# Output projection and query products from two-part operands, low weight parts by GpSimd, in a two-layer trunk on one core

## The chip, the core and the metric

The kernel runs on one core of a Trainium2 chip. The metric is the device time of one execution in microseconds (us), the median of several runs. Engines are named as in the profile: PE is TensorE's matrix product, PEld its weight load, DVE is VectorE, ACT is ScalarE, POOL is GpSimd, SP is SyncE, which issues most transfers. TensorE's granted clock is given as a share of full speed.

## What is computed

The input is 256 tokens of 1024 numbers, with 16 learned tokens in front: 272 tokens. Two layers follow, all in float32. In short:

```
def mixer(x):
    h = rmsnorm(x, mix_g);  z = h @ w_in                 # 1024 -> 3488
    y_conv = silu(layernorm(depthwise_conv31(glu(z)))) @ w_conv_out
    y_mla  = chunk_causal_attention(q, k, v) @ w_mla_out # 8 heads, 96 per head
    merged = sigmoid(g1) * y_conv + sigmoid(g2) * y_mla
    return x + merged @ w_out                            # output projection

def peer(hf):                                            # hf = rmsnorm(x, ffn_g)
    q = (hf @ wq).reshape(T, 8, 2, 128)                  # query products
    s = einsum('thpd,hpnd->thpn', q, keys)               # 128 keys per half
    sv, si = top_k(s, 16)                                # per half
    cand = sums of the two halves (16 x 16);  top_s, pos = top_k(cand, 16)
    ids = si[0] * 128 + si[1];  gw = softmax(top_s)      # 128 experts per token
    act = gelu(u_table[ids] . hf) * gw
    return sum over the 128 experts of act * v_table[ids]

for layer in range(2):
    x = mixer(x);  x = x + peer(rmsnorm(x, ffn_g))
return x[16:]
```

There are 128 x 128 = 16384 experts; `u_table` and `v_table` have 64 MB each per layer.

## The kernel before, in words

Activations stand transposed: 128 features on the partitions, tokens along the row, as `hT` with 8 chunks of 272 columns. In layer 1 the first 16 tokens are left out where they are no longer needed, so tiles have 256 columns there. The program's order on every engine is the order in which it is written; waits between engines are by semaphore. PSUM tiles named `z` rotate through 3 buffers, `sc` through 2.

Dense weights, and both expert tables, come as a stream of 1 MB transfers from SP into four buffers `wraw`; each holds two tiles of 128x1024, and `next_w` hands out the next one. A buffer is filled again when both of its tiles have been used.

The mixer ends with three groups of products. `half_tile(oo)` and `half_tile(uu)` form the attention's and the convolution's outputs; the latter's loop multiplies and adds the gates (L719, L720) into `xh`. Then come 8 tiles of the output projection: `ztile(t0, xh)` makes 8 products per tile over the 8 chunks (each product of two f32 operands is two instructions in the trace), VectorE adds the result to `hT` (L724), ScalarE forms `xg`, `hT` times a gain (`scaled`, L167), and a square (L171), VectorE adds up the squares (L173).

The query loop (16 tiles, from L889) multiplies `xg` with `wq`. ScalarE takes each tile out of PSUM as `qr` (L892). After tile i, TensorE makes the scores of tile i-1 with the keys, and VectorE finds their 16 best (`top16`, five passes, two rows of 128 scores per tile). After tile 1 VectorE computes the inverse norm (`rstd`, L266 and L154 to L159). In tiles 4 to 11 GpSimd multiplies one chunk of `xg` by it and so forms `xh` (L919), the operand of the expert products. From tile 9 on, VectorE works one step per tile at `second`, which finds the best 16 of the sums for the first four heads of the first 128 tokens. After the loop it does the next four heads; then the table `ew` of expert numbers goes out and GpSimd can issue the first gathers.

The experts are computed in two ways. For the last 160 tokens all experts are computed densely: 128 tiles `A` (this is the u stage), GELU, times a matrix `X` of weights that is built on the way from one-hot products (`wbuild`, 40 blocks of 4 tokens), then 128 tiles `po` with `v_table` (the v stage). For the first 96 tokens, and in layer 0 the 16 learned ones, u and v rows are gathered by expert number (1 MB per gather, 112 gathers in layer 0 and 96 in layer 1) and multiplied on VectorE (L1138, L1122).

In the u stage two side programs advance with the tiles: `gathers` by `RU` steps per tile, and `b_`, which runs the routing of the second 128 tokens and then `wbuild`. `b_` takes `RB` = 0.75 steps per tile while it routes, and `RW` steps per tile once it builds weights. In `routes`, `LAG` steps stand before four transposes (L1031) that turn `ef`, the expert numbers and weights, for `wbuild`; the second half of the tokens comes last.

Of the kernel before, what the change touches and what calls it, by code (L numbers as in the profile page):

```python
# [35 lines left out]
RB = 0.75  # L36
RW = (0.52, 0.47)
C_MIX, C_FFN, C_CW, C_CB, C_LG, C_LB, C_QA, C_KVA, C_QN, C_KN = 0, 8, 16, 140, 144, 148, 152, 154, 155, 156
# [5 lines left out]
def trunk_kernel(ctx: ExitStack, tc: tile.TileContext, a: dict, out: bass.AP, dbg=None, stop=None):  # L44
# [124 lines left out]
    def square(sq, c, c0):  # L169

        S.activation(sq[:, c, c0:], hT[:, c, c0:], AF.Square)  # L171
        if c:
            V.tensor_add(sq[:, 0, c0:], sq[:, 0, c0:], sq[:, c, c0:])  # L173

    carry = None
    for l in range(NL):
# [74 lines left out]
        def ztile2():  # L251

            ws = [next_w(), next_w()]
            ps = [zp.tile([128, 512], F32, name="z", bufs=3) for _ in range(2)]
            for c in range(8):
                for w_, p in zip(ws, ps):
                    mm(p[:, :T], w_[:, c * 128:(c + 1) * 128], xg[:, c], c == 0, c == 7)
            return [p[:, :T] for p in ps]

        def sums(dst, src, n):  # L260
# [451 lines left out]

        xh = pp.tile([128, 8, T], F32, name="xh")
        for i in range(4):
            ps = half_tile(uu)
            for f in range(2):
                c = 2 * i + f
                mg = mp.tile([128, T], F32, name="az", bufs=2)
                V.tensor_mul(mg[:, :TQ], gt[0][:, c, t0:], ps[f])  # L719
                V.tensor_add(xh[:, c, t0:], mg[:, :TQ], gt[1][:, c, t0:])  # L720
        xg, sq = big("xg", [8, T]), big("sq", [8, T])
        for i in range(8):
            p = ztile(t0, xh)
            V.tensor_add(hT[:, i, t0:], hT[:, i, t0:], p)  # L724
            scaled(xg, l, i, C_FFN, t0)
            square(sq, i, t0)
# [162 lines left out]
        for i in range(16):  # L889
            z = ztile(t0)  # L890
            qT_ = mp.tile([128, T], F32, name="qr", bufs=2)
# [25 lines left out]
            if 4 <= i < 12:  # L917
                c = i - 4
                G.tensor_tensor(xh[:, c, t0:], xg[:, c, t0:], rs, op=OP.mult)  # L919
        scores(15, pend)  # L920
# [83 lines left out]
        def routes():  # L1004
# [5 lines left out]
            for k in range(2):  # L1010
# [10 lines left out]
                if k == 0:  # L1021
                    if not last:
# [3 lines left out]
                        V.scalar_tensor_tensor(iww[-1].bitcast(I32)[:, 0, 0], im[:, 0], 128.0, im[:, 1], op0=OP.mult, op1=OP.add)  # L1026
                for _ in range(LAG + (7 if last and k == 0 else 0)):
                    yield
# [314 lines left out]
```

## Time and profile before

| | |
|---|---|
| median of 3 runs | 1809.7 us (1806.8 to 1811.29) |
| profiled execution | 1810.55 us, span 1808.8 us, mean granted clock 0.991 |
| PE busy | 1760.8 us (97%) |
| DVE, ACT, POOL busy | 1144.0 us (63%), 423.1 us (23%), 336.4 us (19%) |
| moved by DMA | 559.37 MB, mean 309 GB/s |

| stage | layer 0, from us | layer 1, from us |
|---|---|---|
| output projection | 198.15 | 1112.10 |
| u stage, expert products `A` | 303.08 | 1203.93 |
| routing out, first transfer `iww<-ew` | 321.10 | 1222.81 |

A row of the timeline gives start, length and engine, the line of the kernel and the operation, what is written and read, shape, count, and in brackets the idle time before it with what ended it. Rows of matrix products overlap at their ends, so the pace is read from starts. A row by form gives count, busy time and the mean length in ns. A busy TensorE is not one at its peak, since the length of a product is modelled.

### The profile page before, as it was taken

To read this page: it belongs to the slowest core of one execution; us is meant where nothing else is said; L and a number is where in the kernel's file an instruction comes from. 1 tells how busy PE (TensorE), PEld (TensorE's weight loads), DVE (VectorE), ACT (ScalarE), POOL (GpSimd) and SP (SyncE) were. 2 spreads that over 40 slices of the span, in tenths; PEclk is the share of its full clock that TensorE was granted. 3 is DMA by queue.
4 is the path that set the end of the run, shared out by engine and by line. 5 is a ranking of instruction groups with operands and counts; after the bars stand their busy time and mean duration, and the time that the engine had idled before them with its cause. 6 is when DMAs were issued, how large, how long until landed. Compare 5 with 4: busy or idle time off the path is not lost.

```text
span 1808.8 us, 29412 instructions
## 1 busy us (share of the span) xinstructions
PE 1760.8 (97%) x11611; PEld 1626.7 (90%) x11611; DVE 1144.0 (63%) x3101; ACT 423.1 (23%) x1233; POOL 336.4 (19%) x393
## 2 busy tenths in 40 slices
PE   9999999979999999999999999999899999999998
PEld 7678888979999999999996888899799999999998
DVE  5587358898888654544535764596878886444441
ACT  3443102324444100000014331132244431000000
POOL 0121010122111222333200220102211122322210
PEclk9999999989999999999999999999899999999999
DMA  6123433999999999999961224449999999999993
GB/s 228 70 94 117 157 123 141 367 373 423 424 423 424 424 424 421 424 422 417 422 232 70 94 103 153 163 161 382 366 424 424 423 423 418 421 412 402 421 412 146
DMA packets 80682, 559.37 MB, mean 309 GB/s; under 512 B 9176, under 2 KB 12120, under 8 KB 13080
## 3 DMA queue, kind: packets, MB, share of 16 engines
q1 hardware_dynamic: 49488, 338.54, 46.5%
q0 software_dynamic: 30336, 218.35, 29.1%
q8 instruction: 91, 1.49, 0.3%
q10 hardware_dynamic: 720, 0.60, 0.1%
q14 instruction: 47, 0.39, 0.1%
HBM read 556.18 MB, written 1.05 MB: 308 GB/s over the span
## 4 chain that ended last, share of the span: by engine, by line
PE 73%; DMA 15%; issue 6%; DVE 5%; ACT 0%; POOL 0%; SPq 0%; POOLq 0%; DVEq 0%; ACTq 0%
PE po L52 22%; PE A L52 21%; PE z L52 21%; DMA wraw<-vn 10%; PE aps L52 5%; DMA gb<-uv,iww 3%; PE wp L52 2%; DMA wraw<-u 1%; DVE va L1122 1%; DVE gb L1138 1%; DMA iww<-ew 0%; DVE ex L866 0%; PE xp L52 0%; PE sc L52 0%; DMA wraw<-w_in 0%
## 5 line engine op out<-in xcount | busy, mean ns | idle before, releaser
L52 PE MATMUL po<-X,wraw 128*128 128x160 f32 x4096 | 570.0, 300 | 14.7 <-DMA wraw<-vn 11.0
L52 PE MATMUL A<-xh,wraw 128*128 128x160 f32 x4096 | 580.9, 302 | 3.3 <-DMA wraw<-u 2.1
L52 PEld LDWEIGHTS po<-X,wraw 128*128 128x128 f32 x4096 | 557.8, 190 | 25.3 <-DMA wraw<-vn 20.3
L52 PEld LDWEIGHTS A<-xh,wraw 128*128 128x128 f32 x4096 | 563.3, 191 | 5.0 <-DMA wraw<-u 2.9
L1138 DVE SCALAR_TENSOR_TENSOR gb<-gb,xr 128x1024 f32<-128x1024 f32 x208 | 254.5, 1223 | 348.0 <-DMA gb<-uv,iww 347.6
L52 PE MATMUL z<-xg,wraw 128*128 128x272 f32 (+1 forms) x1408 | 336.3, 393 | 1.3 <-DMA wraw<-w_in 0.7
L1110 POOL DMA_INDIRECT gb<-uv,iww x208 | 217.4, 1045 | 541.5 <-DVE va L1122 366.1
L52 PEld LDWEIGHTS z<-xg,wraw 128*128 128x128 f32 x1408 | 264.7, 192 | 58.5 <-issue 7.2
L1122 DVE SCALAR_TENSOR_TENSOR va<-gb,am,va 128x1024 f32<-128x1024 f32 x203 | 261.2, 1287 | 7.2
L1148 ACT ACTIVATE am<-am 128x1 f32<-128x1 f32 x208 | 41.4, 199 | 598.2 <-DVE gb L1138 598.1
L1052 ACT ACTIVATE ohA<-ohE,wlo 128x128 f16<-128x128 f16 x320 | 105.4, 427 | 11.0 <-DVE ohE L1049 7.5
L1109 POOL COPY warm<-wraw 1x1 f32<-1x1 f32 x91 | 49.6, 545 | 286.0 <-DMA wraw<-vn 286.0
L577 POOL TENSOR_TENSOR acc<-acc,cp 128x272 f32<-128x272 f32 (+1 forms) x60 | 50.7, 845 | 276.4 <-ACT cp L576 274.1
L569 DVE SCALAR_TENSOR_TENSOR acc<-upad,cols,acc 128x272 f32<-128x272 f32 (+1 forms) x180 | 83.6, 520 | 0.2
L1062 ACT ACTIVATE X<-wp 128x356 f32<-128x356 f32 (+24 forms) x80 | 26.8, 335 | 169.6 <-DVE X L1059 164.7
L1049 DVE TENSOR_TENSOR ohE<-ioh,idxT 128x512 f16<-128x512 f16 x160 | 60.5, 419 | 0.0
L52 PE MATMUL z<-xh,wraw 128*128 128x272 f32 (+1 forms) x256 | 57.3, 386 | 0.0
L52 PEld LDWEIGHTS z<-xh,wraw 128*128 128x128 f32 x256 | 48.6, 190 | 8.3
L52 PE MATMUL wp<-ohE,ohA 128*128 128x128 f16 x640 | 49.9, 219 | 0.0
L52 PEld LDWEIGHTS <-ohA 128*128 128x128 f16 x640 | 43.3, 97 | 3.0
L919 POOL TENSOR_TENSOR xh<-xg,rq_ym 128x272 f32<-128x272 f32 (+1 forms) x16 | 11.3, 742 | 181.8 <-DVE sv L749 93.5
L1059 DVE SCALAR_TENSOR_TENSOR X<-wp,X 128x156 f32<-128x156 f32 (+24 forms) x80 | 38.3, 479 | 6.9 <-PE wp L52 6.6
(302 smaller groups left out, 1248.5 us busy)
## 6 DMA issues: line engine op xcount, KB each, us to landing
wraw<-u SPq DMA_DIRECT2D x128, 1024.0 KB
wraw<-vn SPq DMA_DIRECT2D x128, 1024.0 KB
wraw<-w_in SPq DMA_DIRECT2D x27, 1024.0 KB
wraw<-wq SPq DMA_DIRECT2D x16, 1024.0 KB
wraw<-w_out SPq DMA_DIRECT2D x8, 1024.0 KB
wraw<-w_mla SPq DMA_DIRECT2D x4, 1024.0 KB
wraw<-w_conv SPq DMA_DIRECT2D x4, 1024.0 KB
gb<-uv,iww POOLq DMA_INDIRECT x208
```

The lines of the kernel that those rows point to most:

```text
L52: PE.matmul(o, l, r, start=start, stop=stop, skip_group_check=True)
L569: V.scalar_tensor_tensor(acc[:, c, t0:], u_, weight(c, k), acc[:, c, t0:], op0=OP.mult, op1=OP.add)
L577: G.tensor_tensor(acc[:, 0, t0:], acc[:, 0, t0:], u_[:, t0:], op=OP.add)
L1049: V.tensor_tensor(E[q], ioh[:, None].to_broadcast(full), pairs(q, b), op=OP.is_equal)
L1052: S.activation(A_[1][:, t // 2, :, t % 2], E[0][:, t // 2, :, t % 2], AF.Copy, scale=wlo[:, 4 * b + t:4 * b + t + 1])
L1059: V.scalar_tensor_tensor(X[:, :J, s_], p[:, :, :J].rearrange("p t j -> p j t"), 1.0 / WS, X[:, :J, s_], op0=OP.mult, op1=OP.mult)
L1062: S.activation(X[:, J:, s_], p[:, :, J:].rearrange("p t j -> p j t"), AF.Copy, scale=1.0 / WS)
L1109: G.tensor_copy(warm[0:1], state["w"][0:1, 0:1])
L1110: G.indirect_dma_start(out=g_, out_offset=None, in_=a[f"uv{l}"], in_offset=bass.IndirectOffsetOnAxis(ap=iww[i].bitcast(I32)[:, m // 16, 0, ...
L1122: V.scalar_tensor_tensor(vac[i], r, m_, vac[i], op0=OP.mult, op1=OP.add)
L1138: V.scalar_tensor_tensor(u_, u_, 1.0, xrs[i], op0=OP.mult, op1=OP.mult, accum_out=m_)
L1148: S.activation(m_, m_, AF.Gelu_apprx_tanh)
```

## The change

The output projection and the query products are made by `ztile3` instead of `ztile`. Weights and activations are each split in a high part of type f32r (a float32 rounded to fewer bits by the write) and a low part, the rounded rest. A tile is then 24 products: for each chunk high weights with high and with low activations, and then low weights with high activations.

`split` makes the weights' parts two tiles ahead, in two buffers each: the high part is a copy by ScalarE (128x1024), the low part a subtraction by GpSimd (128x1024). The first two are made in the loop before the output projection, the others behind each tile, 24 in a layer. The activations' parts are made by ScalarE and VectorE: `mgh` and `mgl` from `xh` before the output projection, `xgr` and `xgl` from `hT` behind each of its tiles. The squares go to the buffer `acc` with 4 slots. In the query loop `xh` is now `hT` times the inverse norm on GpSimd, then times the gain on ScalarE (L957). `RW` becomes 0.56 in both layers, and the lag before the transposes 3 + 2 steps (layer 0) or 3 + 9 (layer 1) for the first half of the tokens and 3 + 5 for the second, where it was 3, and 3 + 7 for the first half in layer 1.

```diff
--- before.py
+++ after.py
@@ -34,7 +34,7 @@
 J0 = 8
 LAG = 3
 RB = 0.75
-RW = (0.52, 0.47)
+RW = (0.56, 0.56)
 C_MIX, C_FFN, C_CW, C_CB, C_LG, C_LB, C_QA, C_KVA, C_QN, C_KN = 0, 8, 16, 140, 144, 148, 152, 154, 155, 156
 N_COLS = 157
 QT = ((16, 128), (144, 128), (0, 16))
@@ -168,9 +168,10 @@
 
     def square(sq, c, c0):
 
-        S.activation(sq[:, c, c0:], hT[:, c, c0:], AF.Square)
+        b = c and 1 + (c - 1) % (sq.shape[1] - 1)
+        S.activation(sq[:, b, c0:], hT[:, c, c0:], AF.Square)
         if c:
-            V.tensor_add(sq[:, 0, c0:], sq[:, 0, c0:], sq[:, c, c0:])
+            V.tensor_add(sq[:, 0, c0:], sq[:, 0, c0:], sq[:, b, c0:])
 
     carry = None
     for l in range(NL):
@@ -256,6 +257,32 @@
                 for w_, p in zip(ws, ps):
                     mm(p[:, :T], w_[:, c * 128:(c + 1) * 128], xg[:, c], c == 0, c == 7)
             return [p[:, :T] for p in ps]
+
+        parts = []
+
+        def split():
+
+            w_ = next_w()
+            b = split.n % 2
+            split.n += 1
+            h, lo = split.hs[:, b], split.ls[:, b * 1024:(b + 1) * 1024]
+            S.activation(h, w_, AF.Copy)
+            G.tensor_tensor(lo, w_, h.bitcast(F32), op=OP.subtract)
+            parts.append((h, lo))
+
+        split.n = 0
+
+        def ztile3(xhi, xlo):
+            h, lo = parts.pop(0)
+            p = zp.tile([128, 512], F32, name="z", bufs=3)[:, :TQ]
+            for c in range(8):
+                mm(p, h[:, c * 128:(c + 1) * 128], xhi(c), c == 0, False)
+                mm(p, h[:, c * 128:(c + 1) * 128], xlo(c), False, False)
+            for c in range(8):
+                mm(p, lo[:, c * 128:(c + 1) * 128], xhi(c), False, c == 7)
+            if split.n < 24:
+                split()
+            return p
 
         def sums(dst, src, n):
             for c in range(n):
@@ -711,18 +738,28 @@
         uu = vt["u"]
 
         xh = pp.tile([128, 8, T], F32, name="xh")
+        mgh, mgl = big("xg", [8, T], F32R), big("sq", [8, T], F32R)
+        split.hs = mp.tile([128, 2, 8 * 128], F32, name="wuq").bitcast(F32R)
+        split.ls = mp.tile([128, 8, T], F32, name="kh").bitcast(F32R).rearrange("p a b -> p (a b)")
         for i in range(4):
             ps = half_tile(uu)
+            if i == 3:
+                split()
+                split()
             for f in range(2):
                 c = 2 * i + f
                 mg = mp.tile([128, T], F32, name="az", bufs=2)
                 V.tensor_mul(mg[:, :TQ], gt[0][:, c, t0:], ps[f])
                 V.tensor_add(xh[:, c, t0:], mg[:, :TQ], gt[1][:, c, t0:])
-        xg, sq = big("xg", [8, T]), big("sq", [8, T])
+                S.activation(mgh[:, c, t0:], xh[:, c, t0:], AF.Copy)
+                V.tensor_tensor(mgl[:, c, t0:], xh[:, c, t0:], mgh.bitcast(F32)[:, c, t0:], op=OP.subtract)
+        xgr, xgl, sq = big("g0", [8, T], F32R), big("g1", [8, T], F32R), acc
         for i in range(8):
-            p = ztile(t0, xh)
+            p = ztile3(lambda c: mgh[:, c, t0:], lambda c: mgl[:, c, t0:])
             V.tensor_add(hT[:, i, t0:], hT[:, i, t0:], p)
-            scaled(xg, l, i, C_FFN, t0)
+            scaled(xgr, l, i, C_FFN, t0)
+            V.scalar_tensor_tensor(xgl[:, i, t0:], hT[:, i, t0:], cl[:, C_FFN + i:C_FFN + i + 1],
+                                   xgr.bitcast(F32)[:, i, t0:], op0=OP.mult, op1=OP.subtract)
             square(sq, i, t0)
         if stop == f"mix{l}":
             dump(stop, hT)
@@ -887,7 +924,7 @@
         pend = None
         xh = pp.tile([128, 8, T], F32, name="xh")
         for i in range(16):
-            z = ztile(t0)
+            z = ztile3(lambda c: xgr[:, c, t0:], lambda c: xgl[:, c, t0:])
             qT_ = mp.tile([128, T], F32, name="qr", bufs=2)
             S.activation(qT_[:, t0:], z, AF.Copy)
             if i == 0:
@@ -916,7 +953,8 @@
                 next(early, None)
             if 4 <= i < 12:
                 c = i - 4
-                G.tensor_tensor(xh[:, c, t0:], xg[:, c, t0:], rs, op=OP.mult)
+                G.tensor_tensor(xh[:, c, t0:], hT[:, c, t0:], rs, op=OP.mult)
+                S.activation(xh[:, c, t0:], xh[:, c, t0:], AF.Copy, scale=cl[:, C_FFN + c:C_FFN + c + 1])
         scores(15, pend)
         if not last:
 
@@ -1024,7 +1062,7 @@
                         im = r2.tile([128, 2, 16], F32, name="im")
                         yield from second(mv, mi, 1, rsT[:, 2:3], im, iww[-1][:, :, 1])
                         V.scalar_tensor_tensor(iww[-1].bitcast(I32)[:, 0, 0], im[:, 0], 128.0, im[:, 1], op0=OP.mult, op1=OP.add)
-                for _ in range(LAG + (7 if last and k == 0 else 0)):
+                for _ in range(LAG + (5 if k else 9 if last else 2)):
                     yield
                 p = pW.tile([128, 512], F32, name="wp", bufs=2)
                 for q in range(4):
```

VectorE's rows of two output tiles in layer 0, before: `hT` is the residual stream, `sq` the squares.

```order
L719 TENSOR_TENSOR az<-g_603,z 128x272
L720 TENSOR_TENSOR xh<-az,g_604 128x272
L724 TENSOR_TENSOR hT<-hT,z 128x272 x2
L173 TENSOR_TENSOR sq<-sq 128x272
L724 TENSOR_TENSOR hT<-hT,z 128x272
```

The same place now; `g_1399` and `g_1400` hold the high and low parts of the next operand, `acc` the squares, `xg` and `sq` in the third row the parts of `xh`.

```order
L752 TENSOR_TENSOR az<-g_603,z 128x272
L753 TENSOR_TENSOR xh<-az,g_604 128x272
L755 TENSOR_TENSOR sq<-xh,xg 128x272
L759 TENSOR_TENSOR hT<-hT,z 128x272
L761 SCALAR_TENSOR_TENSOR g_1400<-hT,cols_61,g_1399 128x272
L759 TENSOR_TENSOR hT<-hT,z 128x272
L761 SCALAR_TENSOR_TENSOR g_1400<-hT,cols_61,g_1399 128x272
L174 TENSOR_TENSOR acc<-acc 128x272
```

One operation with two SBUF inputs is new per chunk before the projection, and one per tile in it.

GpSimd's rows from the convolution's last adds to the routing in layer 0, before:

```order
L110 IOTA io 128x128
L577 TENSOR_TENSOR acc<-acc,cp 128x272 x30
L919 TENSOR_TENSOR xh<-xg,rq_ym 128x272 x8
L928 DMA mv<-svm 64x1x16
L928 DMA mi<-sim 64x1x16
```

And now; `kh` holds the low weight parts, `wuq` the high ones.

```order
L110 IOTA io 128x128
L604 TENSOR_TENSOR acc<-acc,cp 128x272 x30
L270 TENSOR_TENSOR kh<-wraw,wuq 128x1024 x15
L956 TENSOR_TENSOR xh<-hT,rq_ym 128x272
L270 TENSOR_TENSOR kh<-wraw,wuq 128x1024
L956 TENSOR_TENSOR xh<-hT,rq_ym 128x272
```

The eight multiplications, which stood together, now stand singly behind a subtraction each.

ScalarE's rows in the query loop of layer 0, before, with `tx` a table for `second`:

```order
L171 ACTIVATE sq<-hT 128x272
L892 ACTIVATE qr<-z 128x272 x10
L811 ACTIVATE tx_1815<-it_1811 128x1024
L811 ACTIVATE tx_1817<-it_1812 128x1024
L892 ACTIVATE qr<-z 128x272 x3
```

And now, tiles 3 to 5:

```order
L929 ACTIVATE qr<-z 128x272
L269 ACTIVATE wuq<-wraw 128x1024
L929 ACTIVATE qr<-z 128x272
L957 ACTIVATE xh<-xh,cols_61 128x272
L269 ACTIVATE wuq<-wraw 128x1024
```

Each copy of high weight parts now stands behind the scaling of the tile before, which waits for GpSimd.

## Rows read from the trace of the kernel before

**Rows 1.** Busy time by engine in stretches; first line names the columns

```profile
core 0: us, PE busy (x) PEld busy (x) DVE busy (x) ACT busy (x) POOL busy (x), PEclk, DMA share, GB/s
...
360.00:380.00 20.00, 18.97 (x140) 18.49 (x139) 18.14 (x68) 4.59 (x8) 3.63 (x3) 1.00 1.01 423
...
380.00:400.00 20.00, 9.89 (x56) 8.92 (x55) 19.03 (x53) 5.34 (x13) 3.62 (x4) 0.71 0.87 351
...
1280.00:1300.00 20.00, 11.43 (x67) 10.48 (x67) 19.04 (x56) 5.02 (x13) 3.81 (x3) 0.74 0.80 325
...
640.00:700.00 60.00, 57.81 (x417) 56.12 (x416) 30.44 (x49) 3.38 (x13) 14.01 (x23) 1.00 1.01 421
...
1550.00:1600.00 50.00, 50.00 (x370) 50.00 (x369) 22.40 (x36) 1.83 (x9) 15.43 (x18) 1.00 1.01 422
...
235.92:320.44 84.52, 83.94 (x447) 70.16 (x447) 69.80 (x414) 14.44 (x31) 10.05 (x16) 1.00 0.38 138
```

**Rows 2.** TensorE in order of time: start, length, what, count, idle before

```profile
198.15 29.50 PE L52 MATMUL z<-xh,wraw 128*128 128x272 f32 x128
...
236.15 3.93 PE L52 MATMUL z<-xg,wraw 128*128 128x272 f32 x16
...
240.80 3.94 PE L52 MATMUL z<-xg,wraw 128*128 128x272 f32 x16
...
1112.10 27.79 PE L52 MATMUL z<-xh,wraw 128*128 128x256 f32 x128
...
1151.41 3.62 PE L52 MATMUL z<-xg,wraw 128*128 128x256 f32 x16
...
1155.31 3.62 PE L52 MATMUL z<-xg,wraw 128*128 128x256 f32 x16
```

**Rows 3.** TensorE around the first weight-building products of layer 0

```profile
405.97 0.62 PE L52 MATMUL wp<-ohE,ohA 128*128 128x128 f16 x8
...
406.43 4.56 PE L52 MATMUL A<-xh,wraw 128*128 128x160 f32 x32
```

**Rows 4.** TensorE in layer 1, the four transposes of the second token half

```profile
1290.80 0.45 PE L1031 MATMUL wp<-ident,ef 128*128 128x128 f32 x1 [4.02 <-DVE am L1117]
...
1294.73 0.48 PE L1031 MATMUL wp<-ident,ef 128*128 128x128 f32 x1 [3.48 <-DVE ef L867]
...
1296.27 0.80 PE L1031 MATMUL wp<-ident,ef 128*128 128x128 f32 x2 [1.07 <-DVE ef L1019]
...
1296.86 10.27 PE L52 MATMUL A<-xh,wraw 128*128 128x160 f32 x64
```

**Rows 5.** GpSimd: the multiplications by the inverse norm; below, by form

```profile
243.91 5.78 POOL L919 TENSOR_TENSOR xh<-xg,rq_ym 128x272 f32<-128x272 f32 x8 [93.51 <-DVE sv L749]
...
1155.52 5.51 POOL L919 TENSOR_TENSOR xh<-xg,rq_ym 128x256 f32<-128x256 f32 x8 [88.26 <-ACT qr L892]
...
L577 POOL TENSOR_TENSOR acc<-acc,cp 128x272 f32<-128x272 f32 x30 | 26.0, 868 | 123.1 <-ACT cp L576 122.2
```

**Rows 6.** GpSimd and VectorE at two moments of layer 0, single instructions

```profile
104.61 0.76 POOL L577 TENSOR_TENSOR acc<-acc,cp 128x272 f32<-128x272 f32 x1 [0.35 <-ACT cp L576]
...
104.61 1.06 DVE L569 SCALAR_TENSOR_TENSOR acc<-upad,cols,acc 128x272 f32<-128x272 f32 x1
...
91.67 0.76 POOL L577 TENSOR_TENSOR acc<-acc,cp 128x272 f32<-128x272 f32 x1 [10.13 <-ACT cp L576]
...
91.77 0.44 DVE L677 TENSOR_TENSOR g<-z,rq_ym 128x272 f32<-128x272 f32 x1 [2.41 <-PE z L52]
```

**Rows 7.** VectorE, first and last of the twelve inverse-norm steps, layer 0

```profile
238.31 0.42 DVE L266 TENSOR_SCALAR rq_x<-st 128x272 f32<-128x272 f32 x1
...
243.24 0.44 DVE L159 SCALAR_TENSOR_TENSOR rq_ym<-rq_w,rq_ym 128x272 f32<-128x272 f32 x1
```

**Rows 8.** ScalarE by form: count, busy us, mean ns of one

```profile
L976 ACT ACTIVATE xs<-xh 128x1024 f32<-128x1024 f32 x5 | 5.2, 1045 | 0.0
...
L167 ACT ACTIVATE xg<-hT,cols 128x272 f32<-128x272 f32 x24 | 11.4, 515 | 74.3 <-DVE hT L724 42.2 <-PE po L52 26.2 <-DMA hT<-hT 5.2
```

## The prediction

> **What bounds the kernel now.** I read the table of stretches first. In layer 0 the DMA engines are full from the first expert gathers to the end of the layer: 421 to 423 GB/s, also late, when TensorE has room (640 to 700 us: 417 instructions in 60 us; in layer 1 it does 370 in 50 us, which is its own pace) [rows 1]. So the end of layer 0 is the start of its gathers plus a fixed amount of bytes; the start of the gathers hangs on VectorE's routing, which follows the query products. In layer 1, with 96 gathers for 112, TensorE has no idle time late (50.00 of 50 us) [rows 1], and the end is when the expert products begin plus TensorE's work. In both layers the stage that the diff rewrites (output projection, query products, routing) is serial with what sets the end: a microsecond there is a microsecond of the kernel.
>
> Both layers also have a hole. Near 380 to 400 and 1280 to 1300 us TensorE is busy 9.89 and 11.43 of 20 us, its granted clock falls to 0.71 and 0.74, and the DMA rate drops to 351 and 325 GB/s [rows 1]: in layer 1 the transposes of the second token half wait 4.02, 3.48 and 1.07 us, mostly for VectorE's `ef` [rows 4].
>
> **The matmuls.** An output tile takes 29.34/8 = 3.67 us in layer 0 (27.79/8 = 3.47 in layer 1), as 16 instructions. A query tile with its scores goes every 4.65 us (240.80 - 236.15), in layer 1 every 3.90 [rows 2], so the scores take 0.98 and 0.43. After: 24 instructions per tile, each one part by one part. The trace has no such operand. Its upper neighbour is the f32 instruction of today, 3.67/16 = 229 ns; its lower one the f16 product, 0.46 us for 8 of 128 columns, 57.5 ns [rows 3], so 122 ns for 272 columns and 115 for 256. I take the lower one, since a part is meant to go through once, and keep the upper as a rival. A tile is then 24 x 122 = 2.93 us (2.76), 0.74 us (0.71) less than now, if it is fed. 24 tiles per layer would give 17 to 18 us.
>
> **What feeds them.** Per tile ScalarE copies 128x1024 (1.05 us, the row of `xs` [rows 8]) and GpSimd subtracts 128x1024. GpSimd's 272 and 256 columns take 5.78/8 = 0.722 and 5.51/8 = 0.689 us [rows 5], a slope of 2.06 ns per column; 752 more columns make 0.722 + 1.55 = 2.27 us. Ends: 2.0, if long rows go a little better than that slope; 3.27, the 868 ns of the convolution's adds [rows 5] scaled by 1024/272. I take 2.3, the nearest rows.
>
> That would fit under 2.9 us, but VectorE cannot work freely beside it. At 104.61 us a GpSimd add of 0.76 us and a VectorE operation with two SBUF inputs start together, and the latter takes 1.06 us; a VectorE operation with one input in PSUM, begun 0.10 us into another GpSimd add, takes 0.44 [rows 6]. The row shows 0.6 us lost beside a 0.76 us add, and that the wait ends when the add ends. I carry that over: beside a subtraction of 2.3 us such an operation waits up to 2.3 us, and everything behind it in VectorE's queue too.
>
> The Trainium skill, "SBUF — State Buffer", section "Who interferes with whom", says that a VectorE instruction with two SBUF inputs and a GpSimd instruction that reads SBUF take a shared port in turns, whoever is second waiting for the whole instruction of the other. With no more than the row's 0.6 us lost per subtraction, 24 of them would cost at most 14 us per layer and vanish in VectorE's idle time, and the time would be near the first rival's 1779; by the rule it is up to 2.3 us each, and the sum below. The trace agrees as far as its 0.76 us adds go.
>
> **Sum for layer 0.** (a) Output projection: per tile VectorE adds to `hT`, forms the low part (two SBUF inputs) and adds squares (two SBUF inputs), 0.45 us each by the inverse norm's steps, (243.24 - 238.31)/11 [rows 7]. With the subtraction, turn about: 2.3 + 3 x 0.45 = 3.65, and some 0.25 for the hops to ScalarE and back (estimate): 3.9 against 3.67, so +2 over 8 tiles instead of -6. The first two subtractions fall on the last `xh` and low-part operations, half hidden: +2. The first query tile needs the last low part, behind one more subtraction: +2. Together +6. (b) First four query tiles: 4 x -0.74 = -3. (c) The inverse norm: twelve steps, 5.4 us [rows 7], nine with two SBUF inputs. TensorE keeps ahead and a subtraction runs in each tile, four before it runs dry: 5.4 + 4 x 2.3 = 14.6 us. The first top-16 (2.4 us: 235.92 to 238.31) stands before it, the second behind: 19.4 us, and `scores(3)` needs the PSUM buffer that this second one reads. It is due after 3 x 3.91 = 11.7 us: +7. (d) Tiles 4 to 11: ScalarE's scaling of `xh` waits for GpSimd's multiplication, which stands behind the subtraction, which waits for ScalarE's copy, which stands behind the previous scaling. Once round: 1.05 + 2.3 + 0.72 + 0.5 (`xg`, 515 ns [rows 8]) + 0.3 for hops = 4.9 against 4.65: +2, less the two tiles split during the wait in (c): 0. The copies and subtractions end two tiles early; the last collide with the `second` steps, whose waits fill VectorE's idle time (84.5 - 69.8 = 14.7 us between first score and routing [rows 1]). Layer 0: +6 - 3 + 7 + 0 = +10 us, for TensorE and for the start of the gathers.
>
> **Sum for layer 1.** Fewer columns, faster tiles before, the same subtraction: (a) (3.9 - 3.47) x 8 + 4 = +7; (b) -3; (c) 19 against 3 x 3.19 = 9.6: +9; (d) 8 x (4.9 - 3.9) less the lead: +5. Together +18.
>
> **LAG and RW.** Transposes of the second half come 2 + 5 steps later; at 0.75 steps per tile and 2.2 us per tile that is 20 us, against a wait of 8.6 us [rows 4]. VectorE is at most some 3 us later by the gathers that move ahead. So the hole closes. Layer 0 gets the bytes back: (423 - 351) x 20 us = 1.4 MB, and about half that again while it recovers, 5 us at 423 GB/s. Layer 1 gets 8.6 us, and 10.27 - 64 x 0.1375 = 1.5 us of low clock [rows 4]; I take 9, since DMA runs at 422 GB/s and has little more. Weight building starts 9 tiles later but at 0.56 per tile: 40 blocks in 71 tiles, done by tile 122 of 128. Its cover is those 6 tiles. If the hole stayed, 14 us would be missing.
>
> **Total.** Layer 0 +10 - 5, layer 1 +18 - 9: +14 us on the profiled execution's 1810.55 gives 1824.6; it lies 0.85 over the median, so 1824.
>
> **Rivals.** First, the engines do not exclude each other over a long instruction, or seldom meet. Then (a) -6, (b) -3, (c) nothing, (d) 0, last four tiles -3: -12; layer 1, with the ring of (d) at 4.9 still too slow, -6; LAG -14: 1779. For it: most VectorE work here is top-16, and during the eight multiplications at 243.91 [rows 5] it was not held. Against: rows 6. Second, about 22 subtractions per layer stand on the path (10 in (a), 4 in (c), 8 in (d)); at 2.0 us each the sum falls by 13, to 1811, no change or nearly; at 3.27 it grows by 43, to 1867. Break-even is near 2.0. Third, f32r instructions take the 229 ns of today: a tile is 5.5 us, +1.83 x 48 = 88, which hides the rest: 1884. Speaks for it only that no row shows it otherwise. Fourth, the hole does not close: 1838.
>
> **Chances.** Forecast with its neighbours (subtraction 2.2 to 3.3, hole closed or not) 0.60; no exclusion 0.21; subtraction near 2.0 0.14, mostly within 0.3%; slow f32r 0.05. About 0.3%, 5.4 us, is what a measurement here can tell from no change. Faster 0.24, same 0.12, slower 0.64. Range 1790 to 1858: it reaches into the first rival and to a subtraction of about 3.1 us.
>
> **What would show it.** The rows of `kh<-wraw,wuq` on GpSimd: 2.3 us. VectorE's low parts (`g<-hT,cols,g`) and inverse-norm steps well over 0.45 us, ending with a subtraction: right; all at 0.45: the first rival. TensorE's gaps in the query tiles ending with GpSimd, ScalarE or VectorE. Instructions of a tile 115 to 122 ns apart. No gap before the `ef` transposes. The gathers of layer 0 start 10 us later, the expert products of layer 1 18 us later within their layer. I am wrong if the query stage gets shorter in both layers.

## The result, and the profile after

The changed kernel takes 1824.8 us (median of 4 runs, 1823.2 to 1828.0), beside 1810.5 us for the kernel before on the same chip: the ratio is 1.0081, 95% interval 1.0064 to 1.0099. The forecast was 1824. The time came out as predicted, but not by the steps: the query stage cost about 10 us less than forecast, and the later transposes saved nothing where 14 us were forecast. The two misses cancel, which is luck.

The profiled execution has a span of 1826.2 us, 17.4 more than before; it was the longest of the four (1828.0 us), and the medians differ by 14.3. Where the 17.4 us arise is seen from the first gather of each layer. In the rows below, from GpSimd's timeline, the first two are the kernel before and the others, in a fence of their own, the changed one.

```profile
326.12 1.03 POOL L1110 DMA_INDIRECT gb<-uv,iww  x1 [4.46 <-DMA iww<-ew]
...
1226.78 1.00 POOL L1110 DMA_INDIRECT gb<-uv,iww  x1 [3.33 <-DMA iww<-ew]
```

The timeline of GpSimd after, with two subtractions of the inverse norm's time and a pair from query tiles of layer 1:

```profile
241.08 2.50 POOL L270 TENSOR_TENSOR kh<-wraw,wuq 128x1024 fp32r<-128x1024 f32 x1 [1.59 <-ACT wuq L269]
...
245.07 2.50 POOL L270 TENSOR_TENSOR kh<-wraw,wuq 128x1024 fp32r<-128x1024 f32 x1 [1.49 <-ACT wuq L269]
...
328.94 1.03 POOL L1148 DMA_INDIRECT gb<-uv,iww  x1 [3.97 <-DMA iww<-ew]
...
1187.06 2.40 POOL L270 TENSOR_TENSOR kh<-wraw,wuq 128x1024 fp32r<-128x1024 f32 x1 [1.62 <-issue]
1189.41 0.74 POOL L956 TENSOR_TENSOR xh<-hT,rq_ym 128x256 f32<-128x256 f32 x1
...
1243.30 1.00 POOL L1148 DMA_INDIRECT gb<-uv,iww  x1 [4.21 <-DMA iww<-ew]
```

TensorE's timeline has the first product of layer 1, here before:

```profile
929.36 11.27 PE L52 MATMUL z<-xg,wraw 128*128 128x272 f32 x48 [0.66 <-ACT xg L167]
```

and after:

```profile
931.04 11.27 PE L52 MATMUL z<-xg,wraw 128*128 128x272 f32 x48 [0.66 <-ACT xg L167]
```

So layer 0's first gather is 2.8 us later; from it to the layer's end it is 603.2 us before and 602.1 after. In layer 1 the first gather comes 297.4 us behind the layer's start before and 312.3 after, 14.9 later; from it to the end of the span it is 582.0 and 582.9. The sum 2.8 + 14.9 is the whole difference: behind the first gather the two kernels agree within 1.1 us in each layer. Each of these figures is from one execution. e3 and e12 below have the same stage (e12 with 2.2 us of products more ahead of the gather) and give 327.6 and 325.4 us for layer 0's first gather, 313.1 and 309.5 for that of layer 1, so differences of 3 us at the first gather say little.

VectorE's timeline shows what the subtractions do to it (start, length, line, operation, what it waited for):

```profile
240.88 0.44 DVE L157 SCALAR_TENSOR_TENSOR rq_w<-rq_ym 128x272 f32<-128x272 f32 x1
241.35 2.52 DVE L158 TENSOR_TENSOR rq_w<-rq_w,rq_x 128x272 f32<-128x272 f32 x1
243.91 0.44 DVE L159 SCALAR_TENSOR_TENSOR rq_ym<-rq_w,rq_ym 128x272 f32<-128x272 f32 x1
...
245.34 2.52 DVE L159 SCALAR_TENSOR_TENSOR rq_ym<-rq_w,rq_ym 128x272 f32<-128x272 f32 x1
...
290.06 2.41 DVE L877 CAST nf<-po 128x64 f32<-128x64 int32 x1
...
292.86 2.42 DVE L880 SCALAR_TENSOR_TENSOR ra<-nf,ra 128x64 f32<-128x64 f32 x1
```

Put beside GpSimd's rows: the step at 241.35 begins 0.27 us into the subtraction of 241.08 and ends at 243.87, 0.29 after the subtraction's end at 243.58; the step at 245.34 ends 0.29 after the next one. A step that meets none takes 0.44. The last two rows are `second` steps of the routing, and they are held alike.

By form, over the whole span (count, busy us, mean ns, idle before):

```profile
L761 DVE SCALAR_TENSOR_TENSOR g<-hT,cols,g 128x272 fp32r<-128x272 f32 x8 | 14.1, 1765 | 4.7 <-ACT g L167 4.7
...
L159 DVE SCALAR_TENSOR_TENSOR rq_ym<-rq_w,rq_ym 128x256 f32<-128x256 f32 x3 | 5.4, 1793 | 0.1
...
L270 POOL TENSOR_TENSOR kh<-wraw,wuq 128x1024 fp32r<-128x1024 f32 x48 | 116.8, 2434 | 155.9 <-ACT wuq L269 135.2 <-issue 12.9 <-PE z L52 6.9
```

TensorE's timeline has the tiles and the waits that answer to [rows 2] and [rows 4]:

```profile
204.56 0.39 PE L52 MATMUL z<-xg,wuq 128*128 128x272 f32 x1 [2.57 <-ACT xg L754]
...
210.81 0.29 PE L52 MATMUL z<-xg,wuq 128*128 128x272 f32 x1
...
213.81 0.29 PE L52 MATMUL z<-xg,wuq 128*128 128x272 f32 x1
...
250.90 0.68 PE L52 MATMUL sc<-uk,qr 128*128 128x128 f32 x4 [2.08 <-DVE si L790]
...
427.66 1.01 PE L52 MATMUL wp<-ohE,ohA 128*128 128x128 f16 x8 [15.21 <-issue]
...
1144.20 1.06 PE L52 MATMUL z<-g,wuq 128*128 128x256 f32 x2 [2.22 <-ACT g L167]
...
1166.85 1.19 PE L52 MATMUL sc<-uk,qr 128*128 128x128 f32 x4 [6.10 <-DVE si L790]
...
1191.96 0.71 PE L52 MATMUL sc<-uk,qr 128*128 128x128 f32 x4 [1.16 <-ACT qr L929]
1196.68 0.71 PE L52 MATMUL sc<-uk,qr 128*128 128x128 f32 x4 [1.16 <-ACT qr L929]
...
1319.45 0.60 PE L1069 MATMUL wp<-ident,ef 128*128 128x128 f32 x4
1319.89 6.69 PE L52 MATMUL A<-xh,wraw 128*128 128x160 f32 x48
1341.49 1.01 PE L52 MATMUL wp<-ohE,ohA 128*128 128x128 f16 x8 [14.91 <-issue]
1342.30 6.47 PE L52 MATMUL A<-xh,wraw 128*128 128x160 f32 x32
```

Two output tiles start 3.00 us apart. Query tiles of layer 1 come 4.72 us apart, each behind a wait for ScalarE's `qr`. The transposes at 1319.45 wait for nothing now, but 7 us later TensorE stands still for 14.91 us in front of the first weight-building product (in layer 0 for 15.21). "issue" says only that the profile shows no releaser; VectorE's and ScalarE's rows name it. In ScalarE's timeline of layer 1:

```profile
1334.05 0.20 ACT L1186 ACTIVATE am<-am 128x1 f32<-128x1 f32 x1 [4.27 <-DVE gb L1176]
...
1334.61 0.48 ACT L1070 ACTIVATE idxT<-wp 128x384 f16<-128x384 f32 x1
...
1340.76 1.32 ACT L1090 ACTIVATE ohA<-ohE,wlo 128x128 f16<-128x128 f16 x4 [1.59 <-DVE ohE L1087]
```

And in VectorE's:

```profile
1332.78 1.23 DVE L1176 SCALAR_TENSOR_TENSOR gb<-gb,xr 128x1024 f32<-128x1024 f32 x1 [2.30 <-DMA gb<-uv,iww]
...
1340.24 0.81 DVE L1087 TENSOR_TENSOR ohE<-ioh,idxT 128x512 f16<-128x512 f16 x2
```

The copy `idxT` of transposes that TensorE made at 1319 runs at 1334.61, since in ScalarE's order it stands behind three `am` of gathered rows, each of which waits over 4 us for VectorE, and VectorE for the gather's transfer. VectorE makes the first one-hots at 1340.24, ScalarE its part at 1340.76, and TensorE goes on at 1341.49. TensorE had run ahead of the chain of gathers, and here it must wait for it. The table of stretches shows what that means for the transfers:

```profile
core 0: us, PE busy (x) PEld busy (x) DVE busy (x) ACT busy (x) POOL busy (x), PEclk, DMA share, GB/s
...
1280.00:1300.00 20.00, 20.00 (x151) 20.00 (x150) 19.07 (x68) 5.05 (x9) 3.02 (x3) 1.00 1.01 424
1300.00:1345.00 45.00, 30.09 (x215) 29.88 (x214) 34.78 (x94) 11.50 (x30) 9.11 (x9) 0.82 0.97 402
```

The stretch of [rows 1] at 1280 is full now, at 424 GB/s; the next 45 us hold the gap, and the transfers run on at 402.

### The profile page after: what moved, and what is told of

It is laid out like the page before. It is cut to its first block, busy times and chain, and to the rows that moved or that the text cites. A ratio compares the mean times of both kernels' runs of the same rounds, so it can differ in the third digit from the quotient of the medians.

```text
span 1826.2 us, 30397 instructions
## 1 busy us (share of the span) xinstructions
PE 1740.9 (95%) x11995; PEld 1630.4 (89%) x11995; DVE 1203.2 (66%) x3127; ACT 481.8 (26%) x1306; POOL 446.8 (24%) x441
## 3 DMA queue, kind: packets, MB, share of 16 engines
HBM read 556.18 MB, written 1.05 MB: 305 GB/s over the span
## 5 line engine op out<-in xcount | busy, mean ns | idle before, releaser
L1148 POOL DMA_INDIRECT gb<-uv,iww x208 | 222.2, 1068 | 563.3 <-DVE va L1160 423.9
L52 PE MATMUL z<-xg,wraw 128*128 128x272 f32 (+1 forms) x896 | 216.6, 398 | 0.7 <-ACT xg L167 0.7
L52 PEld LDWEIGHTS z<-xg,wraw 128*128 128x128 f32 x896 | 170.7, 194 | 40.6 <-issue 4.9
L270 POOL TENSOR_TENSOR kh<-wraw,wuq 128x1024 fp32r<-128x1024 f32 x48 | 116.8, 2434 | 155.9 <-ACT wuq L269 135.2
L1147 POOL COPY warm<-wraw 1x1 f32<-1x1 f32 x91 | 38.3, 421 | 273.5 <-DMA wraw<-vn 273.5
L52 PE MATMUL z<-g,wuq 128*128 128x272 f32 (+1 forms) x512 | 73.5, 296 | 3.5 <-ACT g L167 2.2
L52 PEld LDWEIGHTS z<-g,wuq 128*128 128x128 f32 x512 | 66.5, 194 | 6.9 <-issue 2.6
L1100 ACT ACTIVATE X<-wp 128x320 f32<-128x320 f32 (+23 forms) x80 | 25.8, 322 | 161.3 <-DVE X L1097 159.5
L269 ACT ACTIVATE wuq<-wraw 128x1024 fp32r<-128x1024 f32 x48 | 50.4, 1053 | 38.3 <-PE z L52 28.0
```

The source lines that it names most:

```text
L52: PE.matmul(o, l, r, start=start, stop=stop, skip_group_check=True)
L269: S.activation(h, w_, AF.Copy)
L270: G.tensor_tensor(lo, w_, h.bitcast(F32), op=OP.subtract)
L1147: G.tensor_copy(warm[0:1], state["w"][0:1, 0:1])
L1148: G.indirect_dma_start(out=g_, out_offset=None, in_=a[f"uv{l}"], in_offset=bass.IndirectOffsetOnAxis(ap=iww[i].bitcast(I32)[:, m // 16, 0, ...
```

## The experiments

Three readings were open. What is the price of the exclusion between GpSimd's long instructions and VectorE, and which places pay it? Does TensorE's gap cost anything (called A below: TensorE bounds layer 1, each idle us counts; B: a layer ends a fixed time after its first gather)? And is there a version that keeps the gain of three products? Ratios are to the kernel before, run on the same chip; medians of that kernel were 1809.9 to 1812.5 us in these runs. Each edit is to the changed kernel, unless said.

**e1.** Without the subtractions.

```diff
-            G.tensor_tensor(lo, w_, h.bitcast(F32), op=OP.subtract)
-            parts.append((h, lo))
+            parts.append((h, h))
```

> Left out: the low part of the weights; GpSimd's 48 subtractions are gone and the third product takes the high part of the weights once more, so TensorE, ScalarE and VectorE do all that they do in the changed kernel. Theory (long GpSimd subtractions hold up VectorE's two-input operations): the low parts g<-hT,cols,g fall from 1.77 us to 0.43 to 0.5 us, the inverse-norm steps from 1.14 to 0.45 us; the gathers of layer 0 start about 14 us earlier than in the changed kernel (324.4 to about 310), those of layer 1 about 20 us earlier in their layer; the time is 1785 to 1798. Rival (VectorE's low parts are long by themselves, for their type or for the wait on ScalarE): they stay above 1 us and the time stays within 6 us of 1824.8.

Measured: 1786.6 us, ratio 0.9860 (0.9843 to 0.9876). VectorE's rows by form:

```profile
L158 DVE TENSOR_TENSOR rq_w<-rq_w,rq_x 128x272 f32<-128x272 f32 x12 | 5.3, 443 | 0.4
L760 DVE SCALAR_TENSOR_TENSOR g<-hT,cols,g 128x272 fp32r<-128x272 f32 x8 | 4.0, 501 | 9.2 <-ACT g L167 9.2
```

The low part takes 501 ns for 1765, an inverse-norm step 443. All waits of TensorE in the query tiles of layer 0 are gone. The subtractions cost 38 us by the medians, 40 by the ratios. That is the hold of VectorE together with the ring of step (d), where ScalarE waits for GpSimd; no wait of TensorE for `kh` shows in the changed kernel. e2 changes the length of the hold.

**e2.** The same subtraction in four pieces.

```diff
-            G.tensor_tensor(lo, w_, h.bitcast(F32), op=OP.subtract)
+            for k in range(0, 1024, 256):
+                G.tensor_tensor(lo[:, k:k + 256], w_[:, k:k + 256], h.bitcast(F32)[:, k:k + 256], op=OP.subtract)
```

> The subtraction of 128x1024 is issued as four of 128x256, so GpSimd is busy longer in sum (about 4 x 0.69 = 2.76 us per tile for 2.43), but lets go of VectorE four times as often. Theory (a VectorE operation waits for the end of the whole GpSimd instruction that is running): no VectorE operation waits over 0.7 us, the low parts g<-hT,cols,g fall from 1.77 to 0.8 to 1.1 us, the inverse-norm steps from 1.14 to about 0.8; the stage gets back a part: 1806 to 1817 us. Rival (what counts is GpSimd's busy time, or VectorE gets its turn only when GpSimd's queue is empty): low parts as long as now or longer, 1824 to 1835.

Measured: 1816.0 us, ratio 1.0024 (1.0011 to 1.0036).

```profile
L762 DVE SCALAR_TENSOR_TENSOR g<-hT,cols,g 128x272 fp32r<-128x272 f32 x8 | 5.7, 708 | 4.7 <-ACT g L167 4.7
...
L271 POOL TENSOR_TENSOR kh<-wraw,wuq 128x256 fp32r<-128x256 f32 x192 | 144.8, 790 | 122.9 <-ACT wuq L269 95.9 <-PE z L52 13.7 <-issue 13.0
```

GpSimd is busy 28 us longer, TensorE's repeated waits for `qr` in layer 1 grow from 1.16 to 1.58 us, and the kernel is faster than with whole subtractions. So it is the length of one instruction that VectorE waits for, not GpSimd's load. The low parts came out shorter than expected (708 ns, 842 in layer 1), but now the additions of squares meet the pieces: 973 ns for 429.

**e3 and e4.** `LAG` and `RW` of before in the changed kernel, and those of the changed kernel in the one before.

```diff
-RW = (0.56, 0.56)
+RW = (0.52, 0.47)
...
-                for _ in range(LAG + (5 if k else 9 if last else 2)):
+                for _ in range(LAG + (7 if last and k == 0 else 0)):
```

> The changed kernel with LAG and RW as before. Theory A (layer 1 is bound by TensorE, so every idle us in front of the expert products counts): the 14.9 us in front of the first wp go, a wait at the second half's ef transposes comes back, longer than before by what VectorE is later: 10 to 14 us; time 1818 to 1825. Theory B (the start of the gathers and the bytes after it set the end in both layers): TensorE's gap moves to ef and the time stays within 2 us of 1824.8 whatever the gap's length. Theory C (the prediction's: the later order saves what the ef transposes waited, 14 us): 1836 to 1842.

> The kernel before with LAG and RW of the changed one. Theory A (as in e3): the wait of 8.6 us at the ef transposes goes, and a gap of 13 to 16 us comes in front of the first wp in both layers; time 1812 to 1818. Theory B: the same gap, time within 2 us of 1810.5. Theory C: no gap, 1796 to 1800.

Measured: e3 1822.9 us, ratio 1.0062 (1.0045 to 1.0078), which can't be told from the changed kernel's 1.0081; e4 1815.0 us, 1.0017 (1.0007 to 1.0027). TensorE in e3, the transposes of layer 1:

```profile
1302.75 0.44 PE L1069 MATMUL wp<-ident,ef 128*128 128x128 f32 x1 [9.10 <-DVE am L1155]
```

and in e4, the first weight-building product of layer 1:

```profile
1331.88 1.01 PE L52 MATMUL wp<-ohE,ohA 128*128 128x128 f16 x8 [10.70 <-issue]
```

The old order has the gap at the transposes, the new one in front of `wp`, in either kernel. The later transposes move the wait and save nothing. Theory C, the prediction's own, is out. Between A and B these two don't decide: e3 fits both, and e4, 2.7 us above its kernel before, lies within A's range and just outside B's. With e10 below there are three pairs of kernels that differ in the order alone. In each the old order has the lower median, by 1.9, 2.7 and 2.2 us; only e4's interval shows it by itself. So the new order probably costs some 2 to 3 us, and why is not shown.

**e12.** The test of A against B: 8.8 us more work for TensorE in each layer, ahead of the gap.

```diff
-            for c in range(8):
+            for c in (list(range(8)) if j in (9, 12, 15, 18) else []) + list(range(8)):
                 mm(A_[:, jj], w_[:, c * 128:(c + 1) * 128], xh[:, c, d0:], c == 0 and jj == 0, c == 7)
```

> The changed kernel, with the products of four expert tiles (j = 9, 12, 15 and 18 of each layer) made twice, the second pass starting the sum anew, so the output stays. That is 4 x 2.2 = 8.8 us more work for TensorE in each layer, all of it behind the first gather and ahead of the gap before the first wp product (14.9 us in layer 1); no transfer is added. Theory B (the gap is TensorE's lead over the chain of gathers, and a layer ends a fixed time after its first gather): the gap shrinks by 8 to 9 us to about 6 in each layer and the time stays within 3 us of the changed kernel. Theory A (TensorE bounds layer 1, its gap is a loss by itself that VectorE and ScalarE bring about by being late relative to TensorE's own steps): the gap stays and the time rises by 9 us (layer 1) to 18 us (both).

Measured: 1824.8 us, ratio 1.0081 (1.0053 to 1.0108), the time of the changed kernel. TensorE in layer 1:

```profile
1336.14 0.87 PE L52 MATMUL wp<-ohE,ohA 128*128 128x128 f16 x8 [2.58 <-issue]
```

The gap fell from 14.91 to 2.58 us (and 0.39 later), and the work was free. In layer 0 it fell less than forecast:

```profile
426.82 1.01 PE L52 MATMUL wp<-ohE,ohA 128*128 128x128 f16 x8 [11.48 <-issue]
```

Both intervals together still allow a rise of some 6 us, but not A's 9 to 18. Two things make the test less clean than planned. One of the four second passes, that of tile 9, falls ahead of the first gather. And the transfer of expert numbers on which the first gather waits took less: 1.63 and 1.60 us of idle time of GpSimd in the two layers for 3.97 and 4.21 in the changed kernel, so the gathers began earlier. From the first gather on, where the other three passes (6.6 us a layer) lie, layer 0 takes 2.0 us more than in the changed kernel and layer 1 0.7 less. So B holds in both layers, within the spread of the table: the gap is TensorE's lead over the chain of gathers. The table shows it over kernels that differ in the query stage, the order or TensorE's work (us, from the timelines; the gap is TensorE's in layer 1, at `ef` or `wp`):

| kernel | first gather, layer 0 | from it to layer 1 | start of layer 1 to first gather | from it to the end | gap |
|---|---|---|---|---|---|
| before | 326.1 | 603.2 | 297.4 | 582.0 | 8.6 |
| after | 328.9 | 602.1 | 312.3 | 582.9 | 14.9 |
| e1 | 310.4 | 604.0 | 285.6 | 585.1 | 11.6 |
| e2 | 323.2 | 601.2 | 305.3 | 584.1 | 10.6 |
| e3 | 327.6 | 598.6 | 313.1 | 582.2 | 13.7 |
| e4 | 327.5 | 605.3 | 299.1 | 584.0 | 10.7 |
| e5 | 322.3 | 602.4 | 308.1 | 584.4 | 15.3 |
| e6 | 333.3 | 602.5 | 308.0 | 584.7 | 12.0 |
| e7 | 320.4 | 603.7 | 305.4 | 582.5 | 15.0 |
| e8 | 320.6 | 603.3 | 301.6 | 583.8 | 14.9 |
| e9 | 317.9 | 603.1 | 296.7 | 582.6 | 14.7 |
| e10 | 321.3 | 601.5 | 296.5 | 581.6 | 13.6 |
| e11 | 325.0 | 599.9 | 294.5 | 583.6 | 9.1 |
| e12 | 325.4 | 604.1 | 309.5 | 582.2 | 3.0 |

The first gather moves by 23 and 27 us over these kernels, the time behind it by 7 and 4. The test says nothing of work behind the gap. There TensorE has hardly any idle time in layer 1, and from its first weight-building product to the end it is 483.9 to 485.2 us in all ten kernels with the new order. That product starts 97 to 101 us behind the first gather. Whether these could be shortened, say with `idxT` copied ahead of the `am` rows in ScalarE's order, was not tried.

**e5.** The ring of step (d) taken apart.

```diff
+            if 5 <= i < 13:
+                G.tensor_tensor(xh[:, i - 5, t0:], hT[:, i - 5, t0:], rs, op=OP.mult)
+            if 6 <= i < 14:
+                c = i - 6
+                S.activation(xh[:, c, t0:], xh[:, c, t0:], AF.Copy, scale=cl[:, C_FFN + c:C_FFN + c + 1])
             z = ztile3(lambda c: xgr[:, c, t0:], lambda c: xgl[:, c, t0:])
...
-            if 4 <= i < 12:
-                c = i - 4
-                G.tensor_tensor(xh[:, c, t0:], hT[:, c, t0:], rs, op=OP.mult)
-                S.activation(xh[:, c, t0:], xh[:, c, t0:], AF.Copy, scale=cl[:, C_FFN + c:C_FFN + c + 1])
```

> The changed kernel with the ring of step (d) taken apart: GpSimd's multiplication of xh stands ahead of the tile's subtraction instead of behind it, and ScalarE's scaling comes one tile later, so that the next copy of weights never waits for a multiplication. All instructions stay. Theory (the ring of copy, subtraction, multiplication and scaling, 1.05 + 2.43 + 0.77 + 0.5 = 4.75 us, paces query tiles 8 to 13, as the waits for qr of 0.5 and 1.2 us say): these waits go, tiles 8 to 13 pace at 4.0 us in layer 0 and 3.3 to 4.0 in layer 1; the gathers start about 3 us earlier in layer 0 and 5 to 7 in layer 1; 1815 to 1819 us. Rival (VectorE's routing is what the start of the gathers hangs on, whatever TensorE's pace): waits for VectorE come in their place, time within 3 us of the changed kernel.

Measured: 1818.4 us, ratio 1.0032 (1.0020 to 1.0045), clear of the changed kernel's interval. The repeated waits for `qr` are gone in layer 0; two of 0.62 and 0.37 us stay in layer 1.

**e6.** All subtractions on VectorE.

```diff
-            G.tensor_tensor(lo, w_, h.bitcast(F32), op=OP.subtract)
+            V.tensor_tensor(lo, w_, h.bitcast(F32), op=OP.subtract)
```

> All 48 subtractions on VectorE instead of GpSimd, in the same places of the program. No long GpSimd instruction is left, but VectorE gets 24 x 1.2 = 29 us more work in each layer and TensorE's operand stands in VectorE's queue. Theory (the exclusion is what GpSimd's subtractions cost, and VectorE had room only in the output projection): low parts at 0.5 us; the query tiles become VectorE's: top-16 work plus 1.2 us per tile, waits of TensorE for kh; 1808 to 1825 us. Rival (only the exclusion counts, VectorE has room): near the run without subtractions, 1790 to 1800.

Measured: 1832.6 us, ratio 1.0124 (1.0104 to 1.0144): worse than both theories gave. VectorE's low parts are at 0.5 us, but TensorE waits for VectorE and ScalarE all over the query tiles, most of all here (layer 0):

```profile
297.43 0.61 PE L52 MATMUL scm<-uk,qr 128*32 128x128 f32 x2 [4.89 <-DVE sim L790]
```

The exclusion is gone and its place is taken by VectorE's own 59.6 us of subtractions. I had undersized how little room its routing leaves.

**e7 and e8.** The ten subtractions issued up to the last output tile on VectorE, behind the addition to `hT`; the rest on GpSimd, whole (e7) or in two pieces (e8); the ring undone.

```diff
+            if split.n <= 10:
+                subs.append((lo, w_, h))
+            else:
+                G.tensor_tensor(lo, w_, h.bitcast(F32), op=OP.subtract)
...
             V.tensor_add(hT[:, i, t0:], hT[:, i, t0:], p)
+            lows()
```

> The first ten subtractions of a layer, which are made during the output projection, on VectorE (each behind the addition to hT), the other fourteen on GpSimd as in the changed kernel, and the ring undone as in e5. Theory: the waits ahead of the second output tile (2.6 us) and the first query tile (1.1 and 2.2) and the low clock behind them go; the wait of scores for VectorE's second top-16 (2.1 and 6.1 us) stays, since the inverse norm still meets GpSimd; the gathers start 5 us (layer 0) and 11 us (layer 1) earlier than in the changed kernel less what VectorE's ten subtractions add; 1807 to 1813. Rival (VectorE becomes late by its 12 us of subtractions): outproj tiles over 3.2 us apart, 1816 or more.

> As e7, with GpSimd's fourteen subtractions as two of 128x512 each, about 1.27 us apiece. Theory (a VectorE operation waits for the whole GpSimd instruction): the waits of the inverse norm are halved, the scores' wait for VectorE falls to about 1 and 3 us; 3 to 5 us below e7: 1803 to 1809. Rival (only GpSimd's sum counts): as e7 or 1 us above.

Measured: e7 1810.0 us, 0.9988 (0.9978 to 0.9997), as expected; e8 1811.0 us, 0.9991 (0.9982 to 1.0001), no better, against the theory. In e8 the scores of layer 1 still wait 5.60 us for VectorE (6.14 in e7): of the nine repeated steps of the inverse norm there, two were held for 2.52 and 2.44 us in e7, and in e8 six for 1.37 to 1.41. With two pieces in a row, a step that gets through after the first meets the second.

**e9 and e10.** As e7 (the edit is to it), with VectorE's share up to query tile 3, so that the inverse norm meets no subtraction, and GpSimd's last ten in four pieces as in e2; e10 has `LAG` and `RW` of before as well, as in e3.

```diff
-            if split.n <= 10:
+            if split.n <= 14:
                 subs.append((lo, w_, h))
+                if split.n > 10:
+                    lows()
```

> As e7, with three differences: VectorE also makes the subtractions issued in query tiles 0 to 3 (fourteen of 24 a layer), so that the inverse norm meets no GpSimd subtraction; GpSimd's last ten go as four of 128x256; the first two stand behind the last operand of the output projection. Theory (what delays the gathers is VectorE held by GpSimd): the inverse norm's steps all near 0.45 us, the scores' wait of 2.1 and 6.1 us falls under 1 us, the wait of the second output tile (2.3 and 2.5) too; first gather near 315 us in layer 0 and 296 us after its start in layer 1; 1795 to 1802 us. Rival (VectorE's own 14 x 1.22 = 17 us a layer make it late by as much): 1808 to 1816.

> e9 with LAG and RW as before the change. Theory B (a layer ends a fixed time after its first gather): the gap moves from in front of wp to the ef transposes, with about the same length; 0 to 4 us below e9 (e3 and e4 showed 2 to 3 for the old order). Theory A (TensorE's gap counts): the gap at ef is as long as TensorE's lead over the gathers, so also no great change, but a shorter gap must show 1:1 in the time.

Measured: e9 1801.7 us, 0.9953 (0.9936 to 0.9971); e10 1799.5 us, 0.9936 (0.9920 to 0.9953). Both beat both kernels; their intervals don't tell them apart. In e9 the inverse norm's steps with two inputs take 425 to 443 ns on the average. In layer 0 TensorE still waits 2.17 us for VectorE at the scores, against the theory. In layer 1 the scores' wait fell from 6.10 to

```profile
1148.42 0.68 PE L52 MATMUL sc<-uk,qr 128*128 128x128 f32 x4 [0.35 <-DVE si L804]
```

**e11.** The output projection alone in three products, its eight subtractions a layer on VectorE; queries, `LAG` and `RW` as before.

```diff
-            if split.n < 24:
+            if split.n < 8:
...
-            z = ztile3(lambda c: xgr[:, c, t0:], lambda c: xgl[:, c, t0:])
+            z = ztile(t0)
```

> The output projection alone in three products, with all its eight subtractions a layer by VectorE; the query products, the square sums' place apart, and LAG and RW as before the change. GpSimd does nothing new. Theory (part (a) of the prediction without exclusion: 24 x 0.122 us for 3.67 and 3.47 per tile): 5 to 6 us shorter in layer 0, 4 to 5 in layer 1, all of it at the start of the gathers: 1800 to 1804 us. Rival (VectorE's routing takes up what TensorE gains): within 3 us of the kernel before.

Measured: 1805.4 us, 0.9968 (0.9957 to 0.9980): a gain, about half of the expected one and outside both ranges. The first gather came 1.2 us earlier in layer 0 and 3.0 in layer 1; where the rest stays was not followed up.

## Why the prediction came out right, and where its steps failed

- **Instructions of f32r.** Right: 3.00 us for 24 of 272 columns is 125 ns each, 122 forecast; 2.84 us per tile in layer 1, 2.76 forecast.
- **Subtraction and copy.** Right: 2.43 us (2.3 forecast, break-even "near 2.0") and 1.05.
- **The exclusion.** Right as carried over from [rows 6], and shown by e1 and e2. The section "Who interferes with whom" of the page "SBUF — State Buffer" of the Trainium skill, by which the one who is second waits for the whole instruction, agrees: the held steps at 241.35 and 245.34 us end 0.29 us after the subtraction.
- **(a), +6 and +7.** Oversized. Output tiles go every 3.00 us, not 3.9: the step "turn about" failed. Subtractions and VectorE's operations don't add up; the addition to `hT` reads PSUM and ran beside the subtraction, and the low part's 1.77 us end with it. What was lost is at the ends: the first output tile starts 1.4 us later in layer 0 and waits 2.6 us ahead of its last chunk, the tile behind that wait runs at a granted clock of 0.59 on the average (205.5 to 209.0 us), so for the most part at the lower level of 1.2 GHz, and the first query tile is held up for 1.1 us (layer 0) and 2.2 (layer 1) ahead of its last high products. This tile is done 2.1 us later than before in layer 0, and 1.9 later within layer 1. Without its own gain of 0.7 us, which (b) counts, that is about +3 in each layer.
- **(b), -3.** Right: query tiles start 3.98 us apart in layer 0, 0.67 less than in [rows 2].
- **(c), +7 and +9.** The wait is where forecast (scores for VectorE's second top-16), at 2.08 and 6.10 us. "A subtraction runs in each tile, four before it runs dry" was oversized: of the nine steps two were held in each layer, and in layer 1 a step ahead of them (2.48 us).
- **(d), ring of 4.9.** Right: 4.72 us in layer 1; taking it apart gave 6 us by the medians, 9 by the ratios (e5).
- **`second`, at no cost.** Failed: "whose waits fill VectorE's idle time". In layer 0 the expert products start 2.4 us earlier than before and the first gather 2.8 us later. VectorE's held steps of 2.4 us, which took 0.19 and 0.23 before, stand ahead of the gather; how much of its delay is theirs was not tested alone.
- **The stage in sum.** +2.8 and +14.9 at the first gather, for +10 and +18; in the profiles of e3 and e12 +1.5 and +15.7, -0.7 and +12.1.
- **LAG and RW, -14.** Failed, and the largest miss. The hole "closes", as forecast, and comes back in front of `wp`. The step that failed is "Layer 0 gets the bytes back ... Layer 1 gets 8.6 us". The hole was read as a loss by itself; it is where TensorE waits for the gathers that set the layer's end. The fourth rival ("the hole does not close", so no gain from the order) was right on the gain, and its 1838 missed by what the stage was oversized.
- **Layer 1's end is "when the expert products begin plus TensorE's work".** Failed (e12): 8.8 us more of that work ahead of the gap changed nothing. That TensorE has no idle time late, in [rows 1], doesn't make its whole work the bound: it is paced at the gap, and has the rest of the layer to do from there.

So 28 us of stage and -14 of order were forecast, where the profile has 17.7 and -0.2: two misses of opposite sign, and the forecast time is owed to that in good part: luck, not the sum. The sign rests on the exclusion, which the runs bear out: with shorter holds (e2) the change costs 0.2% for 0.8, and without the subtractions, and so without the ring too, it is a gain of 1.4%, the first rival's 1779 within 8 us.

## What to carry to other kernels

A gap of an engine is worth something only if the end of the chain that it belongs to moves with it; before counting it, look for a moment from which all versions take equally long (here the first gather), and put work into the gap to see whether it is free. Work given to GpSimd that holds VectorE, as here, is paid by VectorE for as long as one instruction lasts. So cut it in short pieces (four helped in e2, two gave nothing in e8), keep it away from VectorE's serial steps, or give VectorE itself as much as fits in its idle stretches: e9 and e10 did all three. Sums of moves that each rest on an unproved gain can hit the time by accident; single moves, run apart, show which of them pays.

## What the runs showed of the hardware that was not expected

Some of VectorE's operations with one SBUF input are held too: the cast of 128x64 from int32 to f32 at 290.06 us took 2.41 us, and 186 ns on the average before the change, and a `TENSOR_SCALAR` of the inverse norm on whole numbers (L155, 128x256) took 2.48 us in layer 1 and 0.29 before. Its top-16 passes were not: MAX8 on 128x128 took 286 ns from PSUM (`sc`) and 276 ns from SBUF (`tkw`) on the average in the changed kernel's query stage, beside 24 subtractions.
